# One ring of 160 KB per partition with a first load of 64 KB, in place of five buffers of 32 KB, in a 2x2x2 average pooling

## The chip, the cores and the metric

The kernel runs on one core of one Trainium2 chip. The metric is the device time of one execution in microseconds (us). All times below are medians of several runs unless a single run is named.

## The reference, cut to what matters

```python
x = np.random.randn(8, 32, 32, 32, 32).astype(np.float32)   # batch, channels, d, h, w
for i, j, k in all output positions:                        # 16 x 16 x 16
    window = x[:, :, 2*i:2*i+2, 2*j:2*j+2, 2*k:2*k+2]
    result[:, :, i, j, k] = np.mean(window, axis=(-3, -2, -1))
```

The input has 33.55 MB and the output 4.19 MB. Each output needs seven additions and one multiplication. Batch and channel make 256 rows of 128 KB; 128 of them, one per partition, are one half ("t" in the code).

## The kernel before

A plan cuts each row into pieces. A unit is 32 KB of every partition (4 MiB in all); the last two units are loaded as two pieces of 16 KB. KF is 256 floats, that is 1 KB, and all loads and stores are issued by SyncE on one queue.

```python
pool_in = ctx.enter_context(tc.tile_pool(name="pin", bufs=5))     # five buffers of 32 KB
obuf = [pool_out.tile([P, 16 * KF], F32, name=f"obuf{t}") for t in range(2)]
plan = [(0, 0, (32,)), (0, 32, (32,)), (0, 64, (32,)), (0, 96, (32,)),
        (1, 0, (32,)), (1, 32, (32,)), (1, 64, (16, 16)), (1, 96, (16, 16))]

def pool_unit(buf, t, k0, kb):      # VectorE, three instructions, in place
    ...   # add pairs in d  (128x4096 for a whole unit)          L58, after: L59
    ...   # add pairs in w  (128x2048)                           L62, after: L63
    ...   # add pairs in h, times 0.125, into obuf[t] (128x1024) L65, after: L66

for t, k0, parts in plan:
    tin = pool_in.tile([P, 32 * KF], F32, tag="tin", name="tin")
    # one dma_start for each part, then one pool_unit for each part
    ...
for t, k0, kb in [(0, 0, 16), (1, 0, 14), (1, 14, 2)]:            # three stores
    nc.sync.dma_start(out=ov[...], in_=obuf[t][:, k0 * KF:(k0 + kb) * KF])
# (cut: the first load is moved ahead of the opening barrier, the end waits for the stores)
```

## Time and profile before

| | before |
|---|---|
| time, median of the first 3 runs | 91.99 us (91.84 to 92.0) |
| counted span | 86.4 us |
| DMA engines busy | 99.2% |
| VectorE busy | 64.0 us |

The page of the kernel before has these groups of instructions (line, engine, operation, tile, shapes, count; busy us and mean ns of one; idle us ahead of them and the cause) and these DMA issues (count, KB each, median us from issue to landing):

```profile
L58 DVE TENSOR_TENSOR tin<-tin 128x4096 f32<-128x4096 f32 (+1 forms) x10 | 35.7, 3569 | 20.6 <-DMA tin<-in_x_dram 20.6
L62 DVE TENSOR_TENSOR tin<-tin 128x2048 f32<-128x2048 f32 (+1 forms) x10 | 18.6, 1864 | 0.3
L65 DVE CUSTOM_DVE_ANT_1 obuf<-tin 128x1024 f32<-128x1024 f32 (+1 forms) x10 | 10.1, 1011 | 0.3
...
out_dram<-obuf SPq DMA_DIRECT2D x1, 1792.0 KB, 9.1
out_dram<-obuf SPq DMA_DIRECT2D x1, 256.0 KB, 5.4
```

VectorE (DVE) has 20.6 us of idle time, all of it waiting for loads. The last store has only 256 KB and still needs 5.4 us to land: it stands in a queue that is full.

### The profile page before, as it was taken

Reading aid. Unit: us, or ns where it says so; the run is one execution under the profiler, and the core shown is the slowest. Engines: PE = TensorE matmul, PEld = TensorE weight load, DVE = VectorE, ACT = ScalarE, POOL = GpSimd, SP = SyncE. Lnnn points to the kernel's source line nnn. Section 1 sums busy time; section 2 is a strip of 40 time slices with the busy share of each in tenths; the row PEclk is TensorE's granted clock in tenths of the full one; section 3 lists DMA queues with packets and bytes.
Section 4 is the critical chain, followed back from the end, with each engine's and each line's share of the span. In section 5 each row is a group of like instructions: output and inputs, shape, how many; then the busy total and the mean of one; then the engine's idle time right before and its main releaser. Section 6 shows DMA issues by size and latency. Waiting matters only on the chain.

```text
span 86.4 us, 90 instructions
## 1 busy us (share of the span) xinstructions
DVE 64.0 (74%) x40; POOL 0.2 (0%) x4
## 2 busy tenths in 40 slices
DVE  0000039993999749993999749992999999999994
POOL 0000000000000000000000000000000000000000
DMA  8979997999979999799979999799999999998999
GB/s 243 425 319 470 486 470 319 425 486 486 455 319 440 486 486 410 319 486 486 470 319 425 486 486 440 304 470 387 455 402 455 395 455 410 440 425 319 448 432 408
DMA packets 1634, 36.37 MB, mean 421 GB/s; under 512 B 176, under 2 KB 176, under 8 KB 176
## 3 DMA queue, kind: packets, MB, share of 16 engines
q1 hardware_dynamic: 1634, 36.37, 99.2%
HBM read 33.55 MB, written 4.19 MB: 437 GB/s over the span
## 4 chain that ended last, share of the span: by engine, by line
DMA 61%; DVE 37%; issue 0%; DVEq 0%
DMA tin<-in_x_dram 61%; DVE tin L58 21%; DVE tin L62 11%; DVE obuf L65 6%; DVE dummy L65 0%; DVEq L96 0%
## 5 line engine op out<-in xcount | busy, mean ns | idle before, releaser
L58 DVE TENSOR_TENSOR tin<-tin 128x4096 f32<-128x4096 f32 (+1 forms) x10 | 35.7, 3569 | 20.6 <-DMA tin<-in_x_dram 20.6
L62 DVE TENSOR_TENSOR tin<-tin 128x2048 f32<-128x2048 f32 (+1 forms) x10 | 18.6, 1864 | 0.3
L65 DVE CUSTOM_DVE_ANT_1 obuf<-tin 128x1024 f32<-128x1024 f32 (+1 forms) x10 | 10.1, 1011 | 0.3
L65 DVE DVE_READ_ACCUMULATOR2_ANT dummy<- 128x1 f32 x10 | 0.8, 82 | 0.0
L171 POOL MEMSET const-bfloat16-1.0<- 128x1 bf16 x1 | 0.1, 102 | 0.0
L171 POOL MEMSET const-uint8-127<- 128x1 uint8 x1 | 0.1, 101 | 0.0
L171 POOL MEMSET const-float32-1.0<- 128x1 f32 x1 | 0.1, 99 | 0.0
L171 POOL MEMSET const-float32-0.0<- 128x1 f32 x1 | 0.1, 98 | 0.2 <-issue 0.2
## 6 DMA issues: line engine op xcount, KB each, us to landing
tin<-in_x_dram SPq DMA_DIRECT2D x6, 4096.0 KB, 34.9
tin<-in_x_dram SPq DMA_DIRECT2D x4, 2048.0 KB, 38.0
out_dram<-obuf SPq DMA_DIRECT2D x1, 2048.0 KB, 36.4
out_dram<-obuf SPq DMA_DIRECT2D x1, 1792.0 KB, 9.1
out_dram<-obuf SPq DMA_DIRECT2D x1, 256.0 KB, 5.4
```

Of the source, the lines that this page charges most:

```text
L58: nc.vector.tensor_add(out=b.rearrange("p (o e) -> p o e", o=od), in0=a[:, :, 0], in1=a[:, :, 1])
L62: nc.vector.tensor_add(out=c, in0=bv[:, :, 0], in1=bv[:, :, 1])
L65: nc.vector.tensor_tensor_reduce(out=obuf[t][:, o0:o0 + od * 256].rearrange("p (j k) -> p j k", k=16), in0=cv[:, :, 0], in1=cv[:, :, 1], s ...
L171: nc = _bacc.Bacc("TRN2", target_bir_lowering=False, num_devices=1)
```

## The change

Its intent: fewer and larger transfers (eight loads in place of ten, with the first in one descriptor of 64 KB per partition), and one buffer that is used as a ring, whose parts come free one by one. The core of the diff, with cuts marked:

```diff
-    pool_in = ctx.enter_context(tc.tile_pool(name="pin", bufs=5))
+    ring = pool.tile([P, 160 * KF], F32, name="ring")
     plan = [
-        (0, 0, (32,)),
-        (0, 32, (32,)),
-        ...
-        (1, 64, (16, 16)),
-        (1, 96, (16, 16)),
+        (0, 0, 64, 0),          # half, row, KB per partition, place in the ring
+        (0, 64, 32, 64),
+        (0, 96, 32, 96),
+        (1, 0, 32, 128),
+        (1, 32, 32, 0),
+        (1, 64, 32, 32),
+        (1, 96, 16, 64),
+        (1, 112, 16, 80),
     ]
-    for t, k0, parts in plan:
-        ...
+    for t, k0, kb, r0 in plan:
+        nc.sync.dma_start(
+            out=ring[:, r0 * KF:(r0 + kb) * KF],
+            in_=xv[t * P:(t + 1) * P, k0 * KF:(k0 + kb) * KF])
+        for o in range(0, kb, 32):
+            n = min(kb, 32)
+            pool_unit(ring[:, (r0 + o) * KF:(r0 + o + n) * KF], t, k0 + o, n)
```

More of the change, by code (lines that the diff above doesn't have):

```diff
@@ L31, in pool_rows @@
     ov = out.rearrange("b c d h w -> (b c) (d h w)")
-    pool_in = ctx.enter_context(tc.tile_pool(name="pin", bufs=5))
-    pool_out = ctx.enter_context(tc.tile_pool(name="pout", bufs=1))
-    obuf = [pool_out.tile([P, 16 * KF], F32, name=f"obuf{t}") for t in range(2)]
-    dummy = pool_out.tile([P, 1], F32, name="dummy")
+    pool = ctx.enter_context(tc.tile_pool(name="ring", bufs=1))
+    ring = pool.tile([P, 160 * KF], F32, name="ring")
+    obuf = [pool.tile([P, 16 * KF], F32, name=f"obuf{t}") for t in range(2)]
+    dummy = pool.tile([P, 1], F32, name="dummy")
     plan = [
-        (0, 0, (32,)),
-        (0, 32, (32,)),
-        (0, 64, (32,)),
-        (0, 96, (32,)),
-        (1, 0, (32,)),
-        (1, 32, (32,)),
-        (1, 64, (16, 16)),
-        (1, 96, (16, 16)),
+        (0, 0, 64, 0),
[6 more added lines that the diff above has]
+        (1, 112, 16, 80),
     ]
@@ L69, in pool_unit @@
         )
-    for t, k0, parts in plan:
-        tin = pool_in.tile([P, 32 * KF], F32, tag="tin", name="tin")
-        views = []
-        o = 0
-        for kb in parts:
-            v = tin[:, o * KF:(o + kb) * KF]
-            nc.sync.dma_start(
-                out=v, in_=xv[t * P:(t + 1) * P, (k0 + o) * KF:(k0 + o + kb) * KF])
-            views.append((v, k0 + o, kb))
-            o += kb
-        for v, k, kb in views:
-            pool_unit(v, t, k, kb)
+    for t, k0, kb, r0 in plan:
[5 more added lines that the diff above has]
+            pool_unit(ring[:, (r0 + o) * KF:(r0 + o + n) * KF], t, k0 + o, n)
     for t, k0, kb in [(0, 0, 16), (1, 0, 14), (1, 14, 2)]:
```

## The prediction

> **What bounds the kernel now.** I read the page first for the busy shares, then the cut into windows at the start, middle and end, then the timeline of VectorE, and last the packet and landing records of the trace. The page:
>
> ```profile
> span 86.4 us, 90 instructions
> DVE 64.0 (74%) x40; POOL 0.2 (0%) x4
> q1 hardware_dynamic: 1634, 36.37, 99.2%
> HBM read 33.55 MB, written 4.19 MB: 437 GB/s over the span
> DMA 61%; DVE 37%; issue 0%; DVEq 0%
> ```
>
> VectorE is free for a quarter of the span; the 16 DMA engines are busy for 99.2% of it. The chain of waits (fifth line) gives VectorE 37%, but that chain ends at the last counted instruction, and the stores land after it. The windows show it (length, VectorE busy, GpSimd busy, clock, DMA share, GB/s):
>
> ```profile
> 2.00:76.00 74.00, 54.99 (x30) 0.00 (x0) 1.00 1.00 428
> 76.00:80.00 4.00, 3.93 (x5) 0.00 (x0) 1.00 1.00 369
> 80.00:89.00 9.00, 5.10 (x7) 0.00 (x0) 1.00 0.98 421
> 88.00:90.00 2.00, 0.00 (x0) 0.00 (x0) 1.00 0.79 322
> 90.00:92.00 2.00, 0.00 (x0) 0.00 (x0) 1.00 0.01 3
> ```
>
> The DMA engines are full until the stream runs dry near 90 us, 4 us beyond the counted span. In the packet records the first packet starts at 1.02 us, the last ends at 90.25, and chained by time they fill 16 engines with no hole above 0.11 us. The last store's semaphore is complete at 90.60; the measured 91.99 us is that plus 1.39 us. So the time is: start, all bytes at line rate, last receipt. Only a shorter stream, or a hole in it, can move the end.
>
> VectorE waits for loads and then lags behind the stream (start, length; released by the DMA):
>
> ```profile
> 12.11 4.42 DVE L58 TENSOR_TENSOR tin<-tin 128x4096 f32<-128x4096 f32 x1 [12.11 <-DMA tin<-in_x_dram]
> 21.79 4.42 DVE L58 TENSOR_TENSOR tin<-tin 128x4096 f32<-128x4096 f32 x1 [1.67 <-DMA tin<-in_x_dram]
> ...
> 50.93 4.42 DVE L58 TENSOR_TENSOR tin<-tin 128x4096 f32<-128x4096 f32 x1 [1.69 <-DMA tin<-in_x_dram]
> 60.65 4.43 DVE L58 TENSOR_TENSOR tin<-tin 128x4096 f32<-128x4096 f32 x1 [1.70 <-DMA tin<-in_x_dram]
> ...
> 85.12 0.08 DVE L65 DVE_READ_ACCUMULATOR2_ANT dummy<- 128x1 f32 x1
> ```
>
> A 4 MiB load comes every 9.71 us (60.65 - 50.93 = 9.72), a unit of 32 KB per partition costs VectorE 8.04 us (12.11 to 20.15 in the chain), so it waits 1.7 us per unit up to 60.65, and from there runs without a wait until 85.2.
>
> **What the Trainium skill says.** "DMA: Bandwidth & Descriptors", section "Where 436 GB/s comes from", gives 435.2 GB/s as the ceiling of the 16 DMA ports. The trace agrees: a 32 KB packet takes 1213 ns (median), 27.0 GB/s on an engine and 432 on sixteen (the 437 of the page divides all bytes by a span that ends before the last of them). Section "Why small descriptors are slow (HBM only)" says that each packet carries a small fixed cost beside its bytes; I conclude that from 32 KB up there is little left to save. The trace agrees: 16 KB takes 613 ns, so two cost 1226, only 13 ns above one of 32 KB. "Perfetto Trace Analysis", section "Per-engine timelines", says that the profiler's window of a DMA instruction excludes the movement of the data; the trace agrees, the last store's instruction takes 0.33 us and its data land 5.4 us after issue. The section "Why a DMA increments its semaphore by 16 and not by 1" of "DMA: Bandwidth & Descriptors" mentions a trouble with rows longer than 64 KiB per descriptor; at exactly 64 KiB I take one descriptor per partition to be legal, which no run here shows yet.
>
> **The change, part by part.**
> 1. One first load of 64 KB per partition in place of two of 32 KB. Bytes are equal; each engine has 8 fewer data packets and one fewer semaphore write. The landing records price this: full loads land 9.71 us apart (50.91, 60.63), half loads 4.89 (60.63, 65.52, 70.41), so two halves are 9.78. Eight packets and one 9 ns semaphore write saved are worth 0.07 us. If the fixed cost is the same from 32 to 64 KB, this part saves 0.07 us. (By packet durations it would be 8 x 13 ns + 9 ns = 0.11; records overlap by some 3 ns, hence less.)
> 2. The load of (1, 64) goes from two halves to one. Again 8 packets and a semaphore write per engine: 0.07 us.
> 3. The ring of 160 KB has the bytes of the five old buffers. What it adds is finer release, and here no release is late. Before the change the sixth load was issued at 20.15 and started moving only after the first five, near 50. After: VectorE starts at about 21.7, and its order is add unit 0, add unit 1, then both second adds, then the reduction of unit 0. The first part of the ring is free at 21.7 + 2 x 4.44 + 2 x 2.30 + 1.22 = 36.4 us. The second follows one 4.4 us add and a reduction later, near 42.1; the third after 2.3 + 1.2 more, near 45.7. The loads that take these places have to be in the queue by about 50, 60 and 70, so they have over 10 us of room each. Saves nothing, costs nothing.
> 4. The late start. The first data are signalled at 21.77 - 0.07 = 21.70 in place of 12.09, so VectorE gives up 9.6 us. It had 1.7 us of idle time before each of five later units, 8.45 us in all, which it now spends catching up. Units of (0, 0) to (1, 32), six times 8.04, end at 21.72 + 48.24 = 69.96. The seventh unit's data land at 70.41 - 0.14 = 70.27, so it waits 0.3 us; then one full unit and two halves of 4.19 (76.81 to 81.01 in the chain is 4.20): 70.27 + 8.04 + 8.39 = 86.7, against 85.2 now. So VectorE ends 1.5 us later.
> 5. Does that reach the end? The 14-row store is issued after the first half unit, 70.27 + 8.04 + 4.19 = 82.5. An issue on an idle queue took from 0.00 to 1.02 to move its first packet, so 83.5; the queue before it is full until its first packets started, 84.68, less 0.14: 84.54. Room 1.0 us. The last store is issued at 86.7, could move at 87.7, and the queue is full until 88.94 - 0.14 = 88.80. Room 1.1 us. So the delay is hidden.
>
> Sum: 91.99 - 0.07 - 0.07 = 91.85 us.
>
> **The rivals.**
> (a) The tail comes out. VectorE has only about 1 us of room at each of the two last stores. If issue to first packet takes 2 us rather than 1 (the first load's packets began on different engines between 1.02 and 1.95), some engines idle for up to about 0.9 us before one of the stores: at worst 91.85 + 0.9 = 92.75, more likely 92.0. For it: room and latency are of a size. Against: that spread was on a cold queue at the program's start.
> (b) The kernel becomes bound by VectorE, because half of its prefetch head start is gone. Then its end would have to move past 88 us. Its work from 21.7 is 64.7 us, which ends at 86.4 even without the wait: against. It would need 2 us of new waits, for a time near 93.5.
> (c) A 64 KB descriptor is cut in two by the hardware, or moves no better. Then part 1 saves nothing, or only the semaphore write: 91.92. For it: nothing; against: the build shows one row of 65536 bytes per partition.
> (d) Disturbances in the stream. Between 76.9 and 79.1 us 35 packets of 16 KB took 650 to 1180 ns in place of 613, and that half load needed 5.47 us (75.31 to 80.78) in place of 4.89: 0.57 us lost. The first packets of the program took about 1.9 us in place of 1.2. I don't know the cause. If larger packets or the changed order avoid or double the patch, the time is 91.3 or 92.4. This is larger than the effect I predict and sets the width.
> (e) The large gain, 9.7 us or a sensible part of it, from "eight loads instead of ten". It would need the issues to be on the path. They aren't: ten issues of 0.33 to 0.47 us lie ahead of a queue that never empties.
>
> **Range and chances.** The three runs before lie from 91.84 to 92.0. Point 91.85; the tail (a) and the disturbance (d) upward give 92.15, the disturbance absent, in most of it, gives 91.45. Faster by over 2% means below 90.15: the bytes alone need 89.2 us between first and last packet plus 1.0 ahead and 1.7 behind, so 0.01. Slower by over 2% means above 93.8, which only (b) with further waits would bring: 0.02. Within 2%: 0.97.
>
> **What would show it.** In the changed profile: 128 packets of 65536 bytes at about 2413 ns each (1213 + 1200; about 2426 or twice the number of packets would be rival (c)); VectorE's first add near 21.7, one small wait near 70 and no other, its end near 86.7; DMA idle of VectorE about 22.0 us over two waits in place of 20.6 over six; the counted span up by about 1.5 us, to 87.9, although the time doesn't rise; the last store from issue to landing near 3.8 us in place of 5.4; the DMA share at 1.00 up to 89. A hole in the DMA share between 82 and 89 would show (a), VectorE ending past 88 would show (b), and I'd be wrong outright if the landing of the last store were not within half a microsecond of 90.5.

## The result, and the profile after

| | before | after |
|---|---|---|
| time, median of 6 runs each | 91.92 us (91.83 to 92.14) | 92.06 us (91.71 to 92.31) |
| ratio of the fast runs | | 1.001, interval 0.9987 to 1.0034 |
| counted span | 86.4 us | 87.8 us |
| VectorE's last reduction ends | 85.2 us | 86.6 us |
| last store landed on all engines | 90.60 us | 90.61 us |

The kernels are equal within the noise. (The last three rows are of the one profiled execution of each. A transfer has landed when its completion signal is complete; the traces show 16 parts of it, one for each DMA engine.) The page after:

```profile
span 87.8 us, 82 instructions
...
DVE 62.8 (72%) x36; POOL 0.2 (0%) x4
...
q1 hardware_dynamic: 1390, 37.00, 99.3%
...
L59 DVE TENSOR_TENSOR ring<-ring 128x4096 f32<-128x4096 f32 (+1 forms) x9 | 35.4, 3946 | 23.4 <-DMA ring<-in_x_dram 23.4
...
out_dram<-obuf SPq DMA_DIRECT2D x1, 1792.0 KB, 7.6
out_dram<-obuf SPq DMA_DIRECT2D x1, 256.0 KB, 3.9
```

VectorE idles for 23.4 us where it had 20.6, and does 1.2 us less work. The counted span is 1.4 us longer, because it ends near the issue of the last store, and that comes later. The time doesn't follow: the store then spends 3.9 us to its landing in place of 5.4. The lateness has come out of its time in the queue. The windows after (length, VectorE busy, GpSimd busy, clock, DMA share, GB/s):

```profile
2.00:76.00 74.00, 52.30 (x26) 0.00 (x0) 1.00 0.98 421
76.00:80.00 4.00, 4.00 (x3) 0.00 (x0) 1.00 1.00 356
80.00:89.00 9.00, 6.54 (x9) 0.00 (x0) 1.00 0.99 424
88.00:90.00 2.00, 0.00 (x0) 0.00 (x0) 1.00 0.82 335
90.00:92.00 2.00, 0.00 (x0) 0.00 (x0) 1.00 0.01 4
```

They repeat those of before nearly line by line: no hole, and an end at 90. (A packet counts with its start, so shares and rates of short windows can be off by part of a packet; with packets of 64 KB the first 2 us show more than 16 engines can do.) VectorE's timeline after, in lines that answer to those of before:

```profile
21.94 8.76 DVE L59 TENSOR_TENSOR ring<-ring 128x4096 f32<-128x4096 f32 x2 [21.94 <-DMA ring<-in_x_dram]
...
45.12 4.42 DVE L59 TENSOR_TENSOR ring<-ring 128x4096 f32<-128x4096 f32 x1
...
53.05 4.42 DVE L59 TENSOR_TENSOR ring<-ring 128x4096 f32<-128x4096 f32 x1
...
70.48 4.42 DVE L59 TENSOR_TENSOR ring<-ring 128x4096 f32<-128x4096 f32 x1 [1.49 <-DMA ring<-in_x_dram]
...
86.56 0.08 DVE L66 DVE_READ_ACCUMULATOR2_ANT dummy<- 128x1 f32 x1
```

Two waits are left of six: one of 21.9 us for the large first load, one of 1.49 us at the seventh unit, where VectorE has caught up with the stream. Between, units follow each other every 7.93 us (53.05 - 45.12), 0.11 less than the 8.04 of a unit that stands alone, since the first add of the next starts before the reduction of the last has fully ended.

### The profile page after: what moved, and what is told of

Read it like the earlier page. It is cut to its first block, busy times and chain, and to the rows that moved or that the text cites. A ratio compares the mean times of both kernels' runs of the same rounds, so it can differ in the third digit from the quotient of the medians.

```text
span 87.8 us, 82 instructions
## 1 busy us (share of the span) xinstructions
DVE 62.8 (72%) x36; POOL 0.2 (0%) x4
## 4 chain that ended last, share of the span: by engine, by line
DMA 58%; DVE 41%; issue 0%; DVEq 0%
DMA ring<-in_x_dram 58%; DVE ring L59 25%; DVE ring L63 10%; DVE obuf L66 5%; DVE dummy L66 0%; DVEq L92 0%
## 5 line engine op out<-in xcount | busy, mean ns | idle before, releaser
L59 DVE TENSOR_TENSOR ring<-ring 128x4096 f32<-128x4096 f32 (+1 forms) x9 | 35.4, 3946 | 23.4 <-DMA ring<-in_x_dram 23.4
L63 DVE TENSOR_TENSOR ring<-ring 128x2048 f32<-128x2048 f32 (+1 forms) x9 | 18.4, 2052 | 0.2
L66 DVE CUSTOM_DVE_ANT_1 obuf<-ring 128x1024 f32<-128x1024 f32 (+1 forms) x9 | 9.9, 1105 | 0.2
## 6 DMA issues: line engine op xcount, KB each, us to landing
ring<-in_x_dram SPq DMA_DIRECT2D x1, 21.9
```

The lines of the kernel that those rows point to most:

```text
L59: nc.vector.tensor_add(out=b.rearrange("p (o e) -> p o e", o=od), in0=a[:, :, 0], in1=a[:, :, 1])
L63: nc.vector.tensor_add(out=c, in0=bv[:, :, 0], in1=bv[:, :, 1])
L66: nc.vector.tensor_tensor_reduce(out=obuf[t][:, o0:o0 + od * 256].rearrange("p (j k) -> p j k", k=16), in0=cv[:, :, 0], in1=cv[:, :, 1], s ...
```

## The experiments

The theory: the time is the landing of the last store plus a constant, and that landing is set by a DMA stream without holes, so that only its bytes, a small cost per packet, and its disturbances count; VectorE's later end is hidden in the queue. Rivals: the late start of VectorE costs time that the fewer packets give back; or packet size counts for nothing.

The runs were made on several chips, and every run but store_early was timed in the same rounds as the kernel before. One reading holds for all runs. In the 14 traces the time of the profiled execution less the landing of its last store is 1.38 to 1.40 us. So the landing records carry the verdict where the clock's noise doesn't allow one. These are from the trace's semaphore records; "mean" is over the 16 engines, "last" is the slowest; each run has the name under which its expectation is quoted below:

```
                  first 64 KB landed   last load,      last store   time,
                  mean     last        mean, lasted    landed       profiled run
before            21.58    21.77       5.27            90.60        91.99
part2_only        21.54    21.72       5.32            90.36        91.76
before_last8k     21.58    21.76       5.24            90.47        91.87
before_last16x8k  21.54    21.77       5.41            90.69        92.08
after             21.55    21.92       5.45            90.61        92.00
r_after           21.60    21.97       5.36            90.72        92.11
part1_only        21.49    21.75       5.25            90.29        91.68
room_1            21.54    21.79       5.60            90.62        92.01
after_last8k      21.55    21.76       5.28            90.41        91.81
store_4k          21.61    21.75       5.16            90.48        91.88
packets_8k        22.08    22.29       4.97            91.55        92.94
```

**The change once more (r_after).** The same kernel, five rounds.

> The changed kernel once more, to see what repeats. Theory (the stream of bytes sets the time): ratio to before within 0.997 to 1.003, the first load lands between 21.7 and 22.0 us, VectorE ends near 86.6, the last store lands near 90.6. If the slow first packets of the first trace (about 0.7 us over their later 2418 ns) and the patch of slow 16 KB packets at 77 to 79 us are accidents of one execution, they are elsewhere or absent here; if they belong to the program, they are at the same places, within 0.3 us.

It took 92.07 us (91.76 to 92.14) against 91.91 of before, ratio 1.0007, interval 0.999 to 1.0024. Both disturbances came back at the same places: the first packets of 64 KB took up to 3.49 us in place of 2.42, and slow packets stood between 76.8 and 79.5 us. They belong to the program, but their sizes vary from run to run.

**The first load alone (part1_only).**

```diff
# against the changed kernel
-        (1, 64, 32, 32),
+        (1, 64, 16, 32),
+        (1, 80, 16, 48),
```

> Ring and first load of 64 KB per partition, but the load at row 64 of the second half stays two of 16 KB per partition. Theory: worth 0.07 us at most against before (ratio 0.999), not to be told from 1 by the clock; in the trace the last store lands within 0.1 us of the changed kernel's 90.61. Rival (the first large load costs what the merge gains): last store lands 0.1 us or more later than before's 90.60, ratio over 1.001.

It took 91.95 us, ratio 1.0002 (0.9983 to 1.002). The last store of its trace landed at 90.29, earlier than I allowed for either theory; its first load was also the earliest of all. That is scatter. Over the nine traces with packets of 64 KB (six in the table, and the three of room_3, late_start and store_early below) the first 64 KB had landed at 21.57 on the mean engine and at 21.88 on the slowest; over the four with two loads of 32 KB at 21.56 and 21.76. So the first load gains nothing on the mean and loses 0.1 us on the slowest engine, though not in every trace: in four of the nine the slowest engine is at 21.75 to 21.79, as with 32 KB, and in five at 21.91 to 22.08.

**The merge alone (part2_only).**

```diff
# against the kernel before
-        (1, 64, (16, 16)),
+        (1, 64, (32,)),
```

> The kernel before with the two loads of 16 KB per partition at row 64 of the second half merged to one of 32 KB. Theory: 0.07 us less, ratio 0.999; VectorE starts at 12.1 and waits 1.7 us ahead of each of six later units; the seventh unit's data land at 70.35 in place of 70.41. Rival (the two halves bought something, for instance an earlier start of VectorE on the seventh unit): the last store is issued over 1 us later than 85.2, but the end doesn't move. Only a time over 92.3 would say that the halves mattered.

It took 91.98 us, ratio 1.0003 (0.9985 to 1.0022). The seventh unit's data landed at 70.29, where I expected 70.35; before had 70.41. Of these 0.12 us, 0.05 were there before the load in question (60.58 against 60.63 for the sixth), so the merge itself is worth 0.07 us, as predicted. VectorE's last store was issued at 86.5 in place of 85.2, and the end didn't move. The term is real, and too small for the clock.

**The cost of packets, magnified (packets_8k).** Every load is cut into packets of 8 KB by a padding of 32 bytes in the ring.

```diff
# against the changed kernel; CW = 8 * KF + 8
-    ring = pool.tile([P, 160 * KF], F32, name="ring")
+    ring = pool.tile([P, 20 * CW], F32, name="ring")
...
+            out=ring[...].rearrange("p (o w) -> p o w", w=CW)[:, :, :2048],
+            in_=xv[...].rearrange("p (o w) -> p o w", w=2048))
```

> The changed kernel with every load cut into packets of 8 KB (padding of 32 bytes between the pieces in the ring), nothing else changed: 256 load packets per engine in place of 64. Theory (line rate plus a fixed cost of 8 to 13 ns per packet): 192 more packets, 1.5 to 2.5 us more, 93.6 to 94.6 us, every load 0.2 to 0.4 us longer. Rival (packet size is free here, the memory or the port sets the rate): within 0.2 us of 92.06. The slow start: if it is a fixed time before data flow, the first packets of 8 KB take about 0.7 us over their later duration; if it is a share of the packet, far less.

It took 92.93 us, ratio 1.0118 (1.0096 to 1.0141): more than the rival allows, less than I expected. Full loads are 9.91 us apart on the mean engine in place of 9.715, so 24 more packets cost 0.195 us, 8 ns each; 192 of them are 1.54 us, at the low end of my range. The rest of the miss is a gain that I hadn't expected: the slow patch near 78 us is gone. Here is the same window of before, of the changed kernel and of this one:

```profile
77.00:80.00 3.00, 2.96 (x2) 0.00 (x0) 1.00 1.04 371
```

```profile
77.00:80.00 3.00, 3.00 (x3) 0.00 (x0) 1.00 1.01 339
```

```profile
77.00:80.00 3.00, 3.00 (x2) 0.00 (x0) 1.00 1.00 418
```

The engines are busy in all three, but move 371, 339 and 418 GB/s. The last load lasted 5.36 to 5.45 us in the two traces of the changed kernel, where the 16 KB load ahead of it took 4.90, so the patch cost them about 0.5 us, which came back here (4.97 us, with 8 packets more on each engine): 1.54 - 0.5 is 1.04, and the mean landing of the last store is 1.12 later than in those two (91.35 against 90.26 and 90.21). The slow start is a time, not a share: the first packets of 8 KB took up to 1.2 us in place of 0.31, so up to 0.9 us over theirs; those of 64 KB took up to 1.16 us over their 2.42 (in late_start, below).

**Room at the tail, once within and once beyond (room_1, room_3).** VectorE's second add of the last unit is repeated, once or three times, with the same result.

```diff
# against the changed kernel; 2 for room_1, 4 for room_3
-        nc.vector.tensor_add(out=c, in0=bv[:, :, 0], in1=bv[:, :, 1])
+        for _ in range(2 if (t, k0) == (1, 112) else 1):
+            nc.vector.tensor_add(out=c, in0=bv[:, :, 0], in1=bv[:, :, 1])
```

> The changed kernel with VectorE's second add of the last unit done twice (same result, 1.2 us more), so that the last store alone is issued about 87.9 in place of 86.7. Theory (about 1.1 to 1.3 us of room, from an issue that takes 1.0 us to its first packet and a queue that is full until 89.0): no change, or up to 0.2 us more. Rival (issue to first packet takes 2 us, there is no room left): about 1 us more, 93.0.

> The same with three repeats, 3.7 us more, the last store issued about 90.4. Theory: the room of 1.1 to 1.3 us is spent and the rest shows: 92.06 + 3.7 - 1.2 = 94.5, with a hole in the DMA stream of about 2.4 us ahead of the last store. Rival without room: 95.7. If the end depended on the stream of bytes alone: 92.1.

The first took 91.91 us, ratio 0.9989 (0.9962 to 1.0016): its last store was issued 1.14 us later, at 87.82, and nothing came of it. The second took 93.78 us, ratio 1.0195 (1.0171 to 1.0219), with the last store issued at 90.43. The windows of the first kernel, then of the second:

```profile
86.00:88.00 2.00, 1.75 (x3) 0.00 (x0) 1.00 1.04 444
88.00:90.00 2.00, 0.00 (x0) 0.00 (x0) 1.00 0.88 365
90.00:92.00 2.00, 0.00 (x0) 0.00 (x0) 1.00 0.03 10
```

```profile
86.00:88.00 2.00, 1.97 (x2) 0.00 (x0) 1.00 1.02 437
88.00:90.00 2.00, 1.93 (x3) 0.00 (x0) 1.00 0.44 186
90.00:92.00 2.00, 0.41 (x2) 0.00 (x0) 1.00 0.34 130
```

In the second the DMA share falls to 0.44: the queue runs dry, and the store moves alone in the next window. The store was 3.76 us later than in the changed kernel (90.43 - 86.68) and the time 1.72 longer (93.78 - 92.06), so 2.0 us were hidden, against 1.1 to 1.3 that I had expected. Two things explain it. The first packet followed the issue by 0.83 us, not 1.0 (0.84 in the three other issues on a dry queue, one in late_start and two in store_early). And the room is that of the engine that is last: by the packet records the engines ran dry between 88.9 and 89.5 us, and the last of them waited 1.77 us, about what the time grew by.

**The late start doubled (late_start).** Same loads, but a small VectorE instruction makes the first units depend on the second load too.

```diff
# against the changed kernel, ahead of the first two units
+            for r in (0, 32):
+                nc.vector.scalar_tensor_tensor(            # adds 0 x one element of the second load
+                    out=ring[:, r * KF:r * KF + 1], in0=ring[:, 64 * KF:64 * KF + 1],
+                    scalar=0.0, in1=ring[:, r * KF:r * KF + 1], op0=mult, op1=add)
# (cut: the pool_unit calls of the first two units are moved behind this)
```

> The suspected cost doubled: the same loads, but VectorE may not start before the second load has landed too, so it starts 9.7 us later, at 31.6. Theory: the slack of some 1.5 us at the seventh unit and 1.2 us at the last store is far exceeded, VectorE is then never idle and ends at 31.6 + 64 = 95.6; with 3.4 us from there to the end (issue, first packet, last data, receipt, close) 99.0 us. Rival (the time is bytes alone and VectorE is free for a quarter): 92 to 93.

It took 98.06 us, ratio 1.0654 (1.0624 to 1.0684). The one wait of VectorE on loads, and windows:

```profile
DVE ring L80 <- DMA ring<-in_x_dram: 31.8, 1, 31.8
```

```profile
84.00:86.00 2.00, 2.00 (x2) 0.00 (x0) 1.00 0.29 123
86.00:88.00 2.00, 2.00 (x2) 0.00 (x0) 1.00 0.00 0
88.00:90.00 2.00, 1.97 (x4) 0.00 (x0) 1.00 0.00 0
90.00:92.00 2.00, 2.00 (x3) 0.00 (x0) 1.00 0.54 229
...
94.00:96.00 2.00, 0.63 (x2) 0.00 (x0) 1.00 1.00 414
```

Now the picture is turned over: VectorE is full and the DMA engines stand still from about 85 to 91 us. VectorE's last work ended at 94.6, 1 us sooner than I expected, for units in a row cost 7.93 us and not 8.04; the way from there to the end took 3.6 us in this execution (98.19 - 94.6), where I had put down 3.4. So the first 9.7 us of lateness are free, and the next 9.7 cost 6 us.

**Where the slow patch belongs (store_early).** The 2 MiB store is moved ahead of the last two loads.

```diff
# against the changed kernel
+        if (t, k0) == (1, 64):
+            nc.sync.dma_start(out=ov[:P, :], in_=obuf[0][:, :])     # inside the loop, after this load
-    for t, k0, kb in [(0, 0, 16), (1, 0, 14), (1, 14, 2)]:
+    for t, k0, kb in [(1, 0, 14), (1, 14, 2)]:
```

> The changed kernel with the 2 MiB store put ahead of the last two loads, to find what the patch of slow packets at 77 to 79 us belongs to. If to the passage from loads to a store, it lies some 2 to 3 us ahead of the first store packet, near 67 to 69 us, and perhaps again near 82; if to a time since the start, it stays at 77 to 79; if to the addresses of the last quarter of the second half, it goes to 81 to 84 with them. The time gets longer, near 94 to 95, as the last loads land 4.9 us later and VectorE's tail comes out; that isn't the question.

One run, of unknown state, took 93.91 us. Its two windows, and after them the first window as before has it:

```profile
66.00:69.00 3.00, 2.97 (x2) 0.00 (x0) 1.00 1.01 295
77.00:80.00 3.00, 2.29 (x3) 0.00 (x0) 1.00 1.01 431
```

```profile
66.00:69.00 3.00, 3.00 (x2) 0.00 (x0) 1.00 1.01 431
```

The patch moved with the store: 295 GB/s at 66 to 69 us, where one packet on each of the 16 engines took 1.94 to 2.39 us in place of 1.21, and the full 431 at 77 to 80. So neither a time since the start nor the addresses of the last rows make it. It lies some 3 us ahead of the first store that stands in the queue behind loads. This rests on one execution.

**Three attempts to remove it.** The last load in packets of 8 KB, after the change and before it; the first store in packets of 4 KB; then both last loads in packets of 8 KB.

```diff
# after_last8k, before_last8k: the load (1, 112); before_last16x8k: (1, 96) and (1, 112)
+                nc.sync.dma_start(
+                    out=v.rearrange("p (o w) -> p o w", w=2056)[:, :, :2048],
+                    in_=src.rearrange("p (o w) -> p o w", w=2048))
# store_4k: obuf[0] padded, and
+                out=ov[:P, :].rearrange("p (o w) -> p o w", w=1024),
+                in_=obuf[0].rearrange("p (o w) -> p o w", w=1032)[:, :, :1024])
```

> The changed kernel with only the last load (16 KB per partition, the one ahead of the first store) cut into packets of 8 KB. So far the patch of slow packets is in every kernel whose first store is queued behind loads, and moved to 67 us with the store, but it is absent with 8 KB packets. Theory (a store waiting behind a few packets of over 8 KB slows those): no packet in the last load over 1.2 times its usual duration, the last load takes 4.95 us between landings on the mean of the engines (8 packets more, 0.06 us) in place of 5.36 to 5.45, the end 0.3 to 0.5 us earlier: 91.6, ratio 0.995 to 0.998. Rival (the patch was absent for another reason, such as the packets of all the loads before or the way the queue was filled): patch still there, 92.1.

> The same single cut in the kernel before (five buffers, first loads of 32 KB). Theory: the same gain less the 0.06 us of packets, 91.5 to 91.7, ratio 0.995 to 0.998: the candidate that beats both. Rival: 91.9 to 92.0, ratio over 0.999.

> The other side of the passage: the changed kernel with loads unchanged and the first store cut into packets of 4 KB (8 KB being out of reach of the layout). If the size of the waiting store's packets makes the patch, it shrinks or vanishes; the store itself takes 24 more packets per engine at 8 ns, 0.2 us more. So 91.8 to 92.0 if the patch goes, 92.3 if the size of the loads' packets alone counts.

> The kernel before with both last loads (row 96 of the second half, 2 x 16 KB per partition) in packets of 8 KB. The earlier theory, that the packet size of the last load makes the patch, has fallen: it was still there. What remains of it: the size of the packets already passed or queued with it, as in the run with 8 KB throughout. If that theory holds, no slow packets at 77 to 79 us, the last load takes about 4.95 us on the mean of the engines, the last store lands near 90.3, and the time is 91.6 to 91.8, ratio under 0.998: a kernel that beats both. Rival (something else in the all-8 KB run, which stays open): patch still there, 92.0, ratio 0.999 to 1.002. Besides, one more trace of a first load of 32 KB: theory says its slowest engine lands the first 64 KB by 21.72 to 21.77, the mean engine at 21.54 to 21.58.

They took 92.05, 92.00, 91.94 and 91.96 us, with ratios of 0.9993 (0.9967 to 1.0019), 0.9999 (0.9974 to 1.0024), 0.9991 (0.9963 to 1.0019) and 0.9997 (0.9975 to 1.0019). The patch was in all four traces, and the last load lasted 5.28, 5.24, 5.16 and 5.41 us. My theory, that the packet sizes near the passage from loads to stores make the patch, has fallen. That they change its size is not excluded: over its undisturbed length (4.97 us with packets of 8 KB, 4.90 with 16 KB) the last load lost 0.26 to 0.44 us in these four, and 0.35 to 0.70 in the eight traces whose last load and first store are unchanged. The time of store_4k alone, 91.94, would have fitted the theory; the packets show otherwise. Its 24 further packets per engine cost the store 0.10 us (4.98 from the landing before in place of 4.88), 4 ns each and half of what I expected. (In after_last8k the padding reaches 64 bytes into the next place of the ring, so that load was issued at 51.7 us and not 45.2, still over 20 us before its turn in the queue.) Why the run with 8 KB throughout has no patch is open, and no kernel of this study beats the two.

## Why the prediction was right

The class, the range and the mechanism held: 92.06 us lies within 91.45 to 92.15, and the end stayed with the stream of bytes. The small gain did not show: 91.85 against 91.99 is a ratio of 0.9985, just below both intervals of the change (0.9987 to 1.0034 and 0.999 to 1.0024). The range held because the disturbances had set its width; a change that does nothing would have lain in it too (91.92 of before does). By its steps:

1. The first load (0.07 us saved): not there. One descriptor of 64 KB was legal: 128 packets of 65536 bytes, 2418 ns each, where I worked out 2413, so rival (c) is out. The saving per packet is there: 2418 ns against 2 x 1213 is 8 ns, 0.06 us for the 8 packets of an engine. The start takes it back. At the program's start the first packet of nearly every engine is held up, mostly by 0.5 to 1.1 us. Its start plus its time over the usual gives the moment from which it runs as usual: by the packet records 1.80 us on the mean engine over the four traces with 32 KB (1.78 to 1.82) and 1.89 over the nine with 64 KB (1.82 to 1.97), so 0.09 us are lost there. The measured means of the landings are equal, and the slowest engine landed 0.12 us later on average (21.88 against 21.76), where the sum had it 0.07 earlier. Why a larger first packet is held up longer is not shown.
2. The merge (0.07 us saved): right, 0.07 us by the landings of the merge alone.
3. The ring: no release was late (the ring alone was not run; part1_only, which has it, was no slower than before). The fifth load (row 32 of the second half) was issued at 36.3 us, where I had 36.4, and the later ones at 41.8, 44.0 and 45.2.
4. The late start: the first data came at 21.92, not 21.70, but the six units up to the wait took 47.05 us (21.94 to 68.99), not 48.24, since a unit in a row costs 7.93 us and the first three, whose instructions are interleaved, took 23.18 (21.94 to 45.12). The seventh unit's data came at 70.46, not 70.27. So VectorE waited 1.49 us there in place of 0.3. The end is right all the same, 86.6 against 86.7, because that wait ties VectorE to the load, whatever came before.
5. The tail: hidden, as predicted. The room is 2.0 us and not 1.1, mis-sized for the two reasons under the repeats above. So rival (a) was further off than I thought. Rival (b) exists, but a step further on: it took a start another 9.7 us later to bring it about, and then it cost 6 us.

The sum of 91.85 was 0.2 us low. The first term is missing and slightly negative, and rival (d), the disturbances, is the larger thing: the last load, with packets of 16 KB, lasted 5.16 to 5.60 us in the traces with the patch in it, where 4.90 is undisturbed. (The 0.57 us that the prediction put on it is that of the slowest engine; on the mean engine it is 0.37, 5.27 - 4.90.) Their spread alone is three times the 0.14 us predicted. As the interval of the ratio reaches from 0.9987 to 1.0034, neither a gain of 0.1% nor a loss of 0.3% is excluded for the change as a whole.

## What to carry to other kernels

When the DMA engines have no hole from first to last packet, count bytes and packets, not issues: here two fewer loads could bring 8 ns per load packet saved on each engine, and of the two only the merge brought it. An engine that has idle time to give can start later for free, but only until its last result misses the queue that is still full; work out that room before a first load is made larger, since here one step further cost 6%. And take verdicts on tenths of a microsecond from landings of several traces, not from one.

## What the Trainium skill lacked or had wrong

- "DMA: Bandwidth & Descriptors", section "Where 436 GB/s comes from", says that for transfers between HBM and SBUF the HBM side, about 358 GB/s, binds. With one core at work it doesn't: the loads here ran at 432 GB/s (32 KB in 1213 ns on each of 16 engines), near the ceiling of 435 that the same section gives. The section goes on to note a measurement of 425 GB/s near that ceiling, so what it lacks is that its sentence doesn't hold for a core alone.
- The same page, section "Why small descriptors are slow (HBM only)", gives the cost of a packet in cycles, with an example of 256 bytes, and no sum in ns for packets of this size. Here it is 8 ns a packet for loads from 8 KB up (24 more packets, 0.195 us) and 4 ns for a store in packets of 4 KB (24 more, 0.10 us).
- The same page, section "Latency and other measured facts", gives about 600 ns to the first byte of a DMA issued by SyncE. Here the first packet followed the issue by 1.0 us at the program's start and by 0.83 to 0.84 us on a dry queue late in it.
- No page tells that the first packets of a program are held up, here by up to 0.9 us with 8 KB, 1.0 with 32 KB and 1.16 with 64 KB.
- No page tells of the slow packets some 3 us ahead of the first store that is queued behind loads (371 and 339 GB/s for 3 us), nor why they are absent with packets of 8 KB throughout (418 GB/s).
